# A third PSUM bank for attention scores, and one fewer for transposes, in a two-layer decoder kernel

## The chip, the cores and the metric

The kernel runs on one core of a Trainium2 chip. The time is that of the whole launch on the device, in microseconds (us), the median of the runs shown. The core's engines run side by side, each through its own list of instructions in order, and wait for each other by semaphores: TensorE (PE, matmuls and transposes, writing into PSUM), VectorE (DVE), ScalarE (ACT), GpSimd (POOL) and SyncE (SP, which starts transfers here). PSUM has eight banks of 128 x 512 float32 values; a tile that takes a matmul's result takes one bank.

## The reference

Two layers over 512 tokens of width 1024. Each has one input projection, three token mixers whose results are merged by gates, an output projection and a SwiGLU block. Cut to what is computed:

```python
h = rms_norm(x, mix_norm_g[l])
aq, akc, avc, aks, avs, akw, avw, ag, bcq, bckv, bkpe, cg, cx, ma, mb, mc = split(h @ w_in[l])
# A: 8 heads of 64 in 2 groups; compressed blocks (31), selected blocks, window; merged by gates
o_c = softmax(mask_c(q @ k_c.T)) @ v_c       # k_c, v_c: a small MLP over blocks of 32 tokens
o_s = softmax(mask(q_r @ k_s.T)) @ v_s       # q_r, k_s, k_w carry a rotary embedding
o_w = softmax(mask(q_r @ k_w.T)) @ v_w
ya = g0 * o_c + g1 * o_s + g2 * o_w
# B: latent attention: 8 heads of 96, causal, q and k/v from low-rank bcq and bckv
yb = softmax(mask(q_b @ k_b.T)) @ v_b
# C: causal convolution of cx, gated linear recurrence, times gelu(cg)
merged = sigmoid(ma) * (ya @ w_pa[l]) + sigmoid(mb) * (yb @ w_pb[l]) + sigmoid(mc) * (yc @ w_pc[l])
x = x + merged @ w_o[l]
h = rms_norm(x, ffn_norm_g[l])
x = x + (silu(h @ ffn_w1[l]) * (h @ ffn_w3[l])) @ ffn_w2[l]
```

At 512 tokens there are eight blocks to select from and all are taken, so o_s and o_w are both causal attention over all keys.

## The kernel before

Every large product is float32 made of three passes (`mm3`, lines 111 to 115): both operands are split into a high and a low part, and high x high, high x low and low x high are summed in one PSUM bank. `weights` (103 to 109) loads 128 x 512 values of a matrix into `wr` and splits them: ScalarE writes the high part `wh` (L100), VectorE or, through the attention, GpSimd the low part `wl` (L101).

A layer runs through these stages. First, three **blocks** of projections (`block_tm`): each has four tiles, one per 128 tokens, in banks of the tags t, t, s, s, and sums eight chunks k into all four at once. Between the first block and the next, called block 3 here, `b_in` makes its first product in a "t" tile; four products of its second stand ahead of block 3 and the rest behind it. Block 3's four tiles are read by ScalarE (L422, L413, L414) and VectorE (L423). In block 3, `cmp_mlp` has two groups of 16 small products (L461) for the compressed blocks, the first in a "t" tile, the second in an "mm" tile. The rope tables (first layer only) are made on VectorE (L211 to L229) and end in two sines on ScalarE (L231, L232). The third block, block 1 here, follows.

Then the **attention** (`attn`): 16 jobs of A (a head and a branch each) and 8 of B. Each job has three steps of scores into an "s" tile (`st_s`, L748/L749 for A, L113 to L115 for B), which VectorE masks and reduces (L633) and ScalarE exponentiates (L636); VectorE scales the result (L645); three steps of transposes into a "t" tile (`st_t`, L660), which ScalarE (L100) and VectorE (L101) split into two tiles; and the products with the values into the one "o" bank (`st_v`). The transposes of q and k (`tr4`, L544) and the compressed branch use "t" tiles too. Between the steps, `fill` puts other products in small portions (`b_in`, the gates of A, `b_kv`, `b_halfq`, `merge_a`) into "mm" tiles.

After it (`self.wide = True`) come plain products alone: merge B, the recurrence C, merge C, the output projection and SwiGLU. There `ps()` gives each new "mm" tile the next tag of `WIDE`, so that seven banks are used in turn.

The tags and their banks stand in `pbufs` (line 76): two "mm", two "s", three "t", one "o". A tile waits until a bank of its tag is free, that is until all readers of the tile that had it are done. The order of the instructions on each engine isn't that of the code: a scheduler places them by priority, mostly that of the code, among those that it takes to be ready, so that a change of banks moves instructions.

Of the kernel before, what the change touches and what calls it, by code (L numbers as in the profile page):

```python
# [29 lines left out]
TLAG, VLAG = 6, 2  # L30
EB = 79
F0, F1 = 11.5, 2.5
WIDE = ("s", "t", "mm", "t", "s", "mm", "t")
YK, YQ = 1.3, 1.5
KB = 2
NLAG = 4, 4
# [27 lines left out]
class Builder:  # L64
    def __init__(self, ctx, tc, io, layers=L, dbg=None):
        self.tc, self.nc, self.io, self.layers = tc, tc.nc, io, layers
        self.dbg = dbg or {}
        nc = self.nc
        self.V, self.A, self.T = nc.vector, nc.scalar, nc.tensor
        pool = lambda n, b=1, **k: ctx.enter_context(tc.tile_pool(name=n, bufs=b, **k))  # L70
        self.cst, self.sb, self.sm = pool("cst"), pool("sb"), pool("sm", 2)
        self.psum = pool("psum", 1, space=PSUM)
        self.n = 0
        self.bufs = dict(wr=3, wh=4, wl=4, h=16, mg=8, oT=8, cq=10, qk=8, v=8, big=6, pt=5, P0=2, P1=2, P2=2, P3=3, e=3)
        self.pending = False
        self.pbufs = dict(mm=2, s=2, t=3, o=1)
        self.wide, self.turn = False, 0
        self.weng, self.debt, self.mid = None, 0.0, False

# [7 lines left out]
    def ps(self, tag="mm"):  # L87
        if tag == "mm" and self.wide:
            self.turn += 1
            tag = WIDE[self.turn % 7]  # L90
        return self.psum.tile([128, 512], F32, tag=tag, name=self.nm("ps" + tag), bufs=self.pbufs[tag])
# [1233 lines left out]
```

## Time and profile before

| | us |
|---|---|
| median of 3 runs | 1983.79 (1982.91 to 1984.43) |
| the profiled execution | 1982.81 |
| its span in the trace | 1981.0 |
| TensorE busy | 1935.6 |
| VectorE busy | 1319.7 |
| ScalarE busy | 996.6 |
| GpSimd busy | 252.0 |

The profile is of one execution. The span is the time from the first to the last instruction. Times within the trace count from the span's start. A wait is put down to the instruction that came last among those waited for; idle time of an engine that doesn't set the time costs nothing. The first layer's projections take about 0 to 110 us and its attention goes to about 345; the second layer starts shortly before 1000.

### The profile page before, as it was taken

The page shows a single profiled execution, that of the slowest core. Times are in us where ns is not written, and L with a number is a line of the kernel's source. Part 1 is how long each engine was busy: PE and PEld are TensorE (multiplying, and loading weights), DVE is VectorE, ACT ScalarE, POOL GpSimd, SP SyncE. Part 2 cuts the span into 40 slices and gives each one's busy share as a digit, 9 for nine tenths or more (in the row PEclk, how much of TensorE's full clock was granted, in tenths as well). Part 3 has the DMA queues.
Part 4 walks back from the last instruction along what each step waited for, and adds up shares of the span by engine and source line. Part 5 has one row for each costly group of instructions (what it writes and reads, how often), then busy time and mean ns, then how long its engine had stood idle before and what let it go on. Part 6 is the DMA issues. An engine that isn't in the chain of part 4 may idle for free.

```text
span 1981.0 us, 26967 instructions
## 1 busy us (share of the span) xinstructions
PE 1935.6 (98%) x9472; PEld 1627.8 (82%) x9472; DVE 1319.7 (67%) x2783; ACT 996.6 (50%) x1937; POOL 252.0 (13%) x232
## 2 busy tenths in 40 slices
PE   9898999999999999999999899999999999999999
PEld 8777878888888888888888688888888888888887
DVE  8689998788545554455556999878874465534542
ACT  5466776687334332233344577857773343323331
POOL 0453442000000000000004536310000000000000
PEclk9999999999999999999999999999999999999999
DMA  5211101223333223323432111113233322333333
GB/s 159 86 56 34 41 31 43 87 94 104 109 125 101 96 96 93 99 98 96 131 112 93 43 41 44 38 46 100 95 102 119 121 91 100 96 94 99 97 102 100
DMA packets 100519, 173.94 MB, mean 88 GB/s; under 512 B 11936, under 2 KB 26144, under 8 KB 100384
## 3 DMA queue, kind: packets, MB, share of 16 engines
q1 hardware_dynamic: 100384, 172.22, 27.3%
q8 instruction: 74, 1.21, 0.2%
q14 instruction: 61, 0.50, 0.1%
HBM read 167.98 MB, written 4.19 MB: 87 GB/s over the span
## 4 chain that ended last, share of the span: by engine, by line
PE 78%; DVE 8%; ACT 2%; issue 1%; POOL 0%; ACTq 0%; DVEq 0%; POOLq 0%
PE pst L114 9%; PE pst L113 9%; PE pst L115 9%; PE psmm L113 8%; PE psmm L114 8%; PE psmm L115 8%; PE pss L114 7%; PE pss L113 7%; PE pss L115 7%; PE pst L660 1%; DVE P L645 1%; DVE pss L633 1%; PE pso L673 1%; PE pso L674 1%; ACT P L636 1%
## 5 line engine op out<-in xcount | busy, mean ns | idle before, releaser
L100 ACT ACTIVATE wh<-wr 128x512 fp32r<-128x512 f32 (+3 forms) x640 | 387.5, 608 | 698.4 <-PE pst L114 261.0
L101 DVE TENSOR_TENSOR wl<-wr,wh 128x512 fp32r<-128x512 f32 (+2 forms) x526 | 355.1, 676 | 247.5 <-ACT wh L100 242.4
L101 POOL TENSOR_TENSOR wl<-wr,wh 128x512 fp32r<-128x512 f32 (+2 forms) x114 | 138.8, 1224 | 951.8 <-ACT wh L100 935.8
L113 PE MATMUL psmm<-h,wh 128*128 128x512 f32 x600 | 237.2, 395 | 3.7 <-ACT wh L100 2.8
L115 PE MATMUL psmm<-h,wl 128*128 128x512 f32 x600 | 235.2, 392 | 0.6 <-POOL wl L101 0.6
L114 PE MATMUL psmm<-h,wh 128*128 128x512 f32 x600 | 235.0, 392 | 0.0
L113 PE MATMUL pst<-h,wh 128*128 128x512 f32 x512 | 199.8, 390 | 0.0
L114 PE MATMUL pst<-h,wh 128*128 128x512 f32 x512 | 199.3, 389 | 0.0
L115 PE MATMUL pst<-h,wl 128*128 128x512 f32 x512 | 199.3, 389 | 0.0
L113 PEld LDWEIGHTS psmm<-h,wh 128*128 128x128 f32 x600 | 112.9, 188 | 26.4 <-ACT wh L100 3.2
L113 PE MATMUL pss<-h,wh 128*128 128x512 f32 x344 | 134.2, 390 | 0.0
L115 PE MATMUL pss<-h,wl 128*128 128x512 f32 x344 | 133.9, 389 | 0.0
L114 PE MATMUL pss<-h,wh 128*128 128x512 f32 x344 | 133.9, 389 | 0.0
L115 PEld LDWEIGHTS psmm<-h,wl 128*128 128x128 f32 x600 | 112.9, 188 | 24.6 <-POOL wl L101 1.1
L114 PEld LDWEIGHTS psmm<-h,wh 128*128 128x128 f32 x600 | 112.9, 188 | 20.8
L636 ACT ACTIVATE P<-pss,nm 128x512 f32<-128x512 f32 x192 | 100.1, 525 | 55.4 <-DVE nm L633 32.3
L113 PEld LDWEIGHTS pst<-h,wh 128*128 128x128 f32 x512 | 96.1, 188 | 20.2 <-ACT e L984 0.4
L115 PEld LDWEIGHTS pst<-h,wl 128*128 128x128 f32 x512 | 96.1, 188 | 20.1
L114 PEld LDWEIGHTS pst<-h,wh 128*128 128x128 f32 x512 | 96.1, 188 | 19.8
L633 DVE CUSTOM_DVE_ANT_0 pss<-pss,mask 128x512 f32<-128x512 f32 x192 | 93.7, 489 | 7.2 <-PE pss L115 5.8
L660 PE MATMUL pst<-ident,P 128*128 128x128 f32 x480 | 76.6, 274 | 11.5 <-DVE P L645 5.3
L660 PEld LDWEIGHTS pst<-ident,P 128*128 128x128 f32 x480 | 58.2, 141 | 28.1 <-issue 17.8
(423 smaller groups left out, 4303.4 us busy)
## 6 DMA issues: line engine op xcount, KB each, us to landing
wr<-w SPq DMA_DIRECT2D x240, 256.0 KB, 2.6
wr<-wfm SPq DMA_DIRECT2D x188, 256.0 KB, 2.6
wr<-wpc SPq DMA_DIRECT2D x32, 256.0 KB, 2.6
wr<-wo SPq DMA_DIRECT2D x32, 256.0 KB, 2.6
wr<-wb SPq DMA_DIRECT2D x32, 192.0 KB, 2.4
wr<-w SPq DMA_DIRECT2D x32, 192.0 KB, 2.3
mg<-xT SPq DMA_DIRECT2D x16, 256.0 KB, 2.7
wr<-wpa SPq DMA_DIRECT2D x16, 256.0 KB, 2.6
```

Source lines behind the costliest of these rows:

```text
L100: self.A.activation(hi, src, AF.Copy)
L101: (eng or self.V).tensor_tensor(lo, src, hi.bitcast(F32), OP.subtract)
L113: mm(ps, a[0], b[0], start=first, stop=False)
L114: mm(ps, a[0], b[1], start=False, stop=False)
L115: mm(ps, a[1], b[0], start=False, stop=last)
L633: self.V.tensor_tensor_reduce(p[:, :W], p[:, :W], self.mask[:, 512 - W:], 1.0, 3e38, OP.add, OP.min, j.nm[:, i:i + 1])
L636: self.A.activation(j.Pi[i], p[:, :128 * (i + 1)], AF.Exp, bias=j.nm[:, i:i + 1], scale=-1.0, accum_out=j.l[:, i:i + 1])
L645: V.tensor_scalar(j.Pi[i], j.Pi[i], j.gate[:, i:i + 1], j.l[:, i:i + 1], op0=OP.mult, op1=OP.mult)
L660: self.T.transpose(ps[:, c:c + 128], j.Pi[i][:, kt * 128:kt * 128 + 128], self.ident)
L673: T.matmul(o[:, 512 - n:], j.V[kt], h[:, m0:m0 + n], start=j.first and kt == 0, stop=False)
L674: T.matmul(o[:, 512 - n:], j.V[kt], l_[:, m0:m0 + n], start=False, stop=j.last and kt == NT - 1)
```

## The change

One "t" bank becomes an "s" bank, and the walk over the banks for plain products is written for the new numbers (three s, two t, two mm in seven).

```diff
-WIDE = ("s", "t", "mm", "t", "s", "mm", "t")
+WIDE = ("s", "t", "mm", "s", "t", "mm", "s")
...
-        self.pbufs = dict(mm=2, s=2, t=3, o=1)
+        self.pbufs = dict(mm=2, s=3, t=2, o=1)
```

The number of matmuls, evictions and loads stays the same. What moves is their order. On TensorE at the start of block 3 in the first layer (582 to 585 are its tiles, wh_587/wl_588 the weights of its chunk 0, wh_608/wl_609 those of chunk 1; a line with - is the order before, with + the order after):

```order
 L114 MATMUL pst_582<-wl_609,h_121 128x312
 L115 MATMUL pst_582<-wh_608,h_122 128x312
+L113 MATMUL pss_584<-wh_608,h_121 128x312
+L113 MATMUL pst_583<-wh_587,h_79 128x312
+L114 MATMUL pst_583<-wl_588,h_79 128x312
+L115 MATMUL pst_583<-wh_587,h_80 128x312
 L113 MATMUL pst_583<-wh_608,h_121 128x312
 L114 MATMUL pst_583<-wl_609,h_121 128x312
 L115 MATMUL pst_583<-wh_608,h_122 128x312
-L113 MATMUL pss_584<-wh_608,h_121 128x312
 L114 MATMUL pss_584<-wl_609,h_121 128x312
```

The three products of pst_583 with chunk 0 stood right behind those of pst_582 with chunk 0; now they stand behind chunk 1's products of pst_582 and one of pss_584, with 13 matmuls of block 3 ahead of them. The second layer has the same move.

On TensorE behind block 3, among the products of b_in's second tile (psmm_550), the group of the compression product (two rows of eight matmuls, L461):

```order
 L115 MATMUL psmm_550<-h_129,wl_553 128x512
 L113 MATMUL psmm_550<-h_137,wh_552 128x512
+L461 MATMUL pst_686<-pt_475,qk_682 64x62 x8
+L461 MATMUL pst_686<-pt_476,qk_683 64x62 x8
 L114 MATMUL psmm_550<-h_138,wh_552 128x512
 L115 MATMUL psmm_550<-h_137,wl_553 128x512
```

Before, it stood in the middle of block 3, behind chunk 3; now it is behind the whole block and four further products. The second layer has this move too.

On ScalarE around the evictions of block 3, first layer (v, gth and kpe are what ScalarE reads out of the tiles 582 to 585; big_382 and big_384 are the sines of the rope tables; wh_926 and wh_942 are splits of weights for TensorE's next products):

```order
 L465 ACTIVATE cth_787<-psmm_770 64x62
-L231 ACT_TABLE_LOAD
-L231 ACTIVATE big_382<-big_380 128x192
 L100 ACTIVATE wh_926<-wr_925 128x512
-L232 ACTIVATE big_384<-big_380 128x192
-L100 ACTIVATE wh_942<-wr_941 128x384
 L422 ACTIVATE v_832<-pst_582,ny_360 128x4x64
 L422 ACTIVATE v_837<-pst_583,ny_360 128x4x64
-L100 ACTIVATE wh_961<-wr_960 128x384
 L422 ACTIVATE v_842<-pss_584,ny_360 128x4x64
 L413 ACTIVATE gth_830<-pst_582,ny_360 128x24
+L100 ACTIVATE wh_942<-wr_941 128x384
```

The sines stood ahead of the weight splits and evictions; now they stand behind all of them (and so does wh_961). On VectorE, the evictions of block 3 (L423) stood behind L229, the last step of the rope tables' angle; now the first of them stands six steps (L226) ahead of it.

## Rows read from the trace of the kernel before

**Rows 1.** The page's first part: busy us (share of the span) x instructions

```profile
PE 1935.6 (98%) x9472; PEld 1627.8 (82%) x9472; DVE 1319.7 (67%) x2783; ACT 996.6 (50%) x1937; POOL 252.0 (13%) x232
```

**Rows 2.** Busy time by stretch: stretch and us; PE, PEld, DVE, ACT, POOL; clock; DMA

```profile
200.00:250.00 50.00, 47.44 (x289) 42.60 (x287) 49.39 (x158) 37.01 (x98) 25.06 (x27) 1.00 0.13 40
...
400.00:450.00 50.00, 50.00 (x223) 41.40 (x222) 42.40 (x66) 40.40 (x62) 0.00 (x0) 1.00 0.29 97
```

**Rows 3.** Waits of TensorE: engine, line, waited for; us in total, times, longest

```profile
PE pss L748 <- ACT P L636: 10.6, 13, 1.4
```

**Rows 4.** Busy time by stretch, the two attentions

```profile
110.00:300.00 190.00, 171.93 (x1019) 145.54 (x1017) 184.18 (x550) 132.77 (x352) 82.98 (x77) 0.99 0.12 38
1095.00:1250.00 155.00, 144.06 (x842) 122.62 (x841) 147.05 (x464) 105.98 (x277) 76.92 (x71) 0.99 0.14 44
```

**Rows 5.** Timeline, first layer, block 3: start, us, instruction, count [idle before <-releaser]

```profile
43.25 0.30 PE L113 MATMUL pst<-wh,h 128*128 128x312 f32 x1
...
49.02 0.69 DVE L339 TENSOR_TENSOR e<-pst,rsb 128x512 f32<-128x512 f32 x1
...
55.89 2.08 PE L461 MATMUL psmm<-pt,qk 128*64 128x62 f32 x32
```

**Rows 6.** Timeline, first layer, between block 3 and block 1's end

```profile
66.87 0.35 DVE L226 SCALAR_TENSOR_TENSOR big<-pt,big 128x192 f32<-128x192 f32 x1
67.25 0.26 DVE L229 TENSOR_SCALAR big<-big 128x192 f32<-128x192 f32 x1
...
67.55 0.36 ACT L231 ACTIVATE big<-big 128x192 f32<-128x192 f32 x1 [8.02 <-DVE big L229]
...
68.48 0.50 PE L113 MATMUL psmm<-h,wh 128*128 128x512 f32 x1 [2.81 <-ACT wh L100]
...
70.89 0.34 PE L113 MATMUL pst<-wh,h 128*128 128x384 f32 x1
...
85.20 0.33 PE L113 MATMUL pst<-wh,h 128*128 128x384 f32 x1
...
93.52 0.39 PE L113 MATMUL psmm<-h,wh 128*128 128x512 f32 x1
```

**Rows 7.** Busy time by stretch, first layer, block 1

```profile
70.00:75.00 5.00, 3.04 (x12) 2.17 (x13) 4.93 (x12) 2.85 (x12) 2.10 (x3) 0.94 0.41 120
75.00:80.00 5.00, 5.00 (x22) 4.85 (x22) 4.35 (x9) 3.71 (x8) 1.65 (x2) 0.72 0.13 39
```

**Rows 8.** Timeline, second layer, block 3 to block 1

```profile
1035.97 0.30 PE L113 MATMUL pst<-wh,h 128*128 128x312 f32 x1
...
1041.66 0.69 DVE L339 TENSOR_TENSOR e<-pst,rsb 128x512 f32<-128x512 f32 x1
...
1042.69 0.31 PE L115 MATMUL pss<-wh,h 128*128 128x312 f32 x1
...
1054.09 0.39 PE L113 MATMUL psmm<-h,wh 128*128 128x512 f32 x1
...
1057.94 0.39 PE L115 MATMUL psmm<-h,wl 128*128 128x512 f32 x1
...
1058.82 0.86 DVE L423 SCALAR_TENSOR_TENSOR v<-pst,ny,v 128x256 fp32r<-128x256 f32 x2
...
1059.92 0.28 ACT L414 ACTIVATE kpe<-pst,ny 128x32 f32<-128x32 f32 x1
...
1060.28 0.34 PE L113 MATMUL pst<-wh,h 128*128 128x384 f32 x1
...
1061.16 0.44 PE L114 MATMUL pst<-wl,h 128*128 128x384 f32 x1 [0.54 <-POOL wl L101]
...
1068.37 0.44 PE L114 MATMUL pst<-wl,h 128*128 128x384 f32 x1 [0.50 <-POOL wl L101]
```

**Rows 9.** Timeline, first layer, one transpose group and VectorE's end of its eviction

```profile
137.28 0.60 PE L660 MATMUL pst<-ident,P 128*128 128x128 f32 x4
...
142.13 0.63 DVE L101 TENSOR_TENSOR pt<-pst,pt 128x512 fp32r<-128x512 f32 x1
```

## The prediction

> **What bounds the kernel now.** I read the profile from the whole to the place. The page's busy line puts TensorE at 98% of the span [rows 1], so over the whole kernel little but TensorE's own work sets the time. The stages differ, though. In 50 us stretches TensorE is full in the plain products (400 to 450) and not in the attention (200 to 250), where VectorE is busy for 49.39 of 50 us [rows 2]. The attention runs from about 110 to 300 in the first layer and 1095 to 1250 in the second. Over these stretches VectorE is busy for 184.18 of 190 and 147.05 of 155 us, TensorE for 171.93 and 144.06 [rows 4]. So **VectorE carries the attention**: 5.8 and 8.0 us are all that it leaves idle there, while TensorE has 18.1 and 10.9 us to spare. What the change aims at is a line in the list of TensorE's waits: score matmuls (L748) that wait for the exponential (L636) to leave a score bank, 13 times, 10.6 us in all [rows 3].
>
> Ahead of the attention stand three blocks of projections per layer, each in two "t" and two "s" banks. There the order of work shows what the missing third "t" bank does, so the sum is made there.
>
> **The change, part by part.** *Nothing is added or taken away in work*: the same matmuls, evictions and loads run in the same number. The walk over seven banks for plain products meets each bank every seventh tile before and after, and TensorE's order in those stages differs in bank names alone. I cost that part at nothing. Its cover is that each eviction there has six other tiles' time; a walk out of step with its pools would be seen as waits in the stretch that is now 50.00 of 50 us busy [rows 2].
>
> *First wait, block 3.* The tile of b_in's first product (pst_506) and block 3's first two (pst_582, pst_583) had a "t" bank each. With two banks pst_583 must take the one that pst_506 leaves, so its first products now stand behind 13 others. In the first layer block 3 starts at 43.25; a 312-column matmul goes out every 0.143 us (48 from 1035.97 to 1042.69 with the last) [rows 5, 8], so TensorE is there at 43.25 + 13 x 0.143 = 45.1. VectorE reads pst_506 (L339) only at 49.02 and ends at 49.71 [rows 5], as it does its earlier work first in both orders. TensorE waits 4.6 us. In the second layer: there at 1037.8, free at 1041.66 + 0.69 = 1042.35 [rows 8], 4.5 us.
>
> *Second wait, the compression product.* Its group (L461, 2.08 us [rows 5]) had the third bank in the middle of block 3. It now stands behind block 3 and four products of b_in, and needs a bank that block 3 leaves, which is when ScalarE has read the tile for the last time (L414). TensorE gets there, first layer: 49.7 + 83 x 0.143 + one other L461 group of 2.1 + 4 x 0.227 = 64.6; the 0.227 us is from 17 matmuls between 1054.09 and 1057.94 [rows 8]. VectorE's own eviction (L423) comes before ScalarE's last read and has its place six steps of the rope tables (0.36 us each) ahead of L229, which ran at 67.25 [rows 6]: at 65.1 if nothing else moves, at about 68 if the ten small steps now put ahead no longer run between the others. I take 67, nearer to the upper end since those steps depend on each other, plus 1.3 for the eviction, the two reads and a weight split between them on ScalarE. So the group starts at 68.3, after 3.7 us, and the next block (block 1) at 68.3 + 2.1 + 20 x 0.227 = 74.9, where it started at 70.89 [rows 6]: 4.0 later.
>
> *What the first layer gets back.* ScalarE waited 8.02 us for VectorE's angle (L231) with weight splits and evictions queued behind it, and TensorE waited 2.81 us for one of these [rows 6]. In the new order L231 stands behind the evictions. Block 1 took 93.52 - 70.89 = 22.6 us, and at the pace of its undisturbed second half (48 matmuls from 85.20 to 93.52 [rows 6], 0.173 each) 96 take 16.6: 6.0 us of waits and low clock, which the later start gives its weights time to avoid. Of these, 1.7 us are clock: 0.94 and 0.72 of full over two stretches of 5 us, the lower of the two levels for part of them, right after TensorE's waits [rows 7]. A new wait of 3.7 us may bring that again. First layer: 4.0 - 6.0 = -2.0 without, -0.3 with it. I take 0, since that nothing else waits in block 1 is the best case.
>
> *The second layer gets nothing back*, as no rope tables are made there. VectorE's evictions start at 1058.82, ScalarE's last read of the tile ends at 1059.92 + 0.28 [rows 8]; both orders have the same work ahead of them. TensorE is there at 1042.35 + 83 x 0.143 + 2.2 + 0.9 = 1057.3, waits to 1060.2, and starts block 1 at 1060.2 + 2.1 + 4.5 = 1066.8 instead of 1060.28. Waits of 0.54 and 0.50 us in block 1 fall away [rows 8]: **+5.5 us**, or +7.2 with a stretch of low clock. VectorE has nothing to do while block 1 runs, so the whole attention moves by that much.
>
> *The third score bank.* Its bounds are far apart. All 10.6 us of [rows 3] at best; nothing if VectorE is the limit, since a score that is ready sooner is read no sooner; and a loss if two banks hold the transposes back. The nearest row is VectorE's idle time, 5.8 and 8.0 us [rows 4], most of it many short handovers that a bank doesn't shorten. I take -2 for both layers, bounds -10.6 and +8 (the rivals).
> The Trainium skill, page "Perfetto Trace Analysis", section "Identifying Performance Opportunities", speaks against the change: work on the engine that is most contended within the regime, which here is VectorE by [rows 4]. By that rule alone the score bank brings 0 and the sum would be 1989.
>
> **The sum.** 0 + 5.5 - 2 = +3.5 us on the profiled execution of 1982.81 (span 1981.0), 1986.3. The median of the runs, 1983.79, is 1.0 above it, so I forecast **1987** us.
>
> **Rivals.** (a) *The score bank is what TensorE lacks.* All 10.6 us go and the blocks still lose 5.5: 1983.8 - 5.1 = 1978.7. For it: 13 waits on just that bank. Against it: VectorE's 97 and 95%. It decides when VectorE's busy share in the attention rises above these.
> The same page and section of the Trainium skill has the rule for this: gaps that repeat on the engine that should be saturated can mean too little PSUM for the next tile. The trace has the gaps, but on an engine that is not the saturated one there.
>
> (b) *Two banks are too few for the transposes: slower.* Place: the attention of both layers. A transpose group holds its bank from its start on TensorE to the end of VectorE's subtraction (L101), 137.28 to 142.76 in one case, 5.5 us [rows 9]. Three groups per job and about one further "t" tile share two banks, and 16 jobs fill the 190 us, 11.9 each. Up to 2 x 11.9 / 4 = 6.0 us of mean hold cost nothing; above it each 0.1 us lengthens a job by 0.2. At 6.3 that is 0.6 a job, and for about half of 32 jobs 9 us: 1987 + 9 = 1996. For it: 5.5 is close to 6.0. Against it: in the order the transposes move by few places, and holds among the later heads, where VectorE has room, must be shorter.
>
> (c) *The blocks don't lose.* If the evictions of pst_506 and pst_582 come earlier than I place them, the two waits are hidden: 1983.8 - 2 = 1982.
>
> **How the numbers follow.** Chances: forecast 0.50 (its own range 1983 to 1991), (a) 0.18, (b) 0.20, (c) 0.12. A measurement tells 0.2% from no change, 4 us: faster ends at 1979.8, slower begins at 1987.8. Slower: (b) and 0.21 of the forecast, 0.41. Faster: most of (a), 0.16. Same: 0.43. Range: from just under (a) to (b), 1978 to 1996, which leaves about 2 in 10 out.
>
> **What would show it.** Right: TensorE waits of some 4.5 us for L339 in block 3 of both layers; a wait of 2 to 4 us ahead of an L461 group behind block 3; block 1 of the first layer in under 20 us; block 1 of the second layer starting some 6 us later within its layer; the score waits shorter than 10.6 us with VectorE's busy time in the attention and the attention's length nearly as before. Wrong: an attention shorter by more than 5 us in a layer (a), new TensorE waits of transposes (L660, L544) for L101 (b), or no wait in block 3 (c).

## The result, and the profile after

The changed kernel takes **1997.12 us** (median of 4 runs, 1992.99 to 1999.29), the kernel before 1983.94 on the same chip: a ratio of 1.0061 [1.0049, 1.0073], 12 us slower. The forecast was 1987 with a range up to 1996; the time lies 1.1 us above the range. "No change" had a chance of 0.43 and "slower" 0.41; it was slower.

The profiled execution took 1999.29 us, the longest of the four, with a span of 1997.5 us. The busy line of its page, against [rows 1]:

```profile
PE 1948.9 (98%) x9472; PEld 1640.9 (82%) x9472; DVE 1314.7 (66%) x2783; ACT 998.7 (50%) x1937; POOL 253.6 (13%) x232
```

The number of TensorE's instructions is the same and its busy time is 13.3 us longer: products ran for longer. With that goes TensorE's mean granted clock, which fell from 0.997 to 0.989. Its waits (engine, line, waited for; us in total, times, longest), of which [rows 3] showed one line:

```profile
PE pst L660 <- DVE pt L101: 12.6, 8, 3.7
PE pst L113 <- DVE e L339: 8.4, 2, 4.5
PE pst L461 <- ACT kpe L414: 3.0, 1, 3.0
```

The score waits (10.6 us) are gone: no wait of L748 for L636 of 0.3 us or more is left in TensorE's list, as the change meant. In their place stand transposes that wait for VectorE's split (L101), the two waits of block 3 for L339 and one of the compression group for L414.

Busy time by stretch (us; PE, PEld, DVE, ACT, POOL; clock; DMA), the two attentions 7 and 13 us later than in [rows 4], and the 5 us around the end of the wait of block 3 (51.03) or behind it (1049.50):

```profile
117.00:307.00 190.00, 175.47 (x1019) 148.71 (x1018) 180.91 (x550) 134.60 (x352) 83.09 (x77) 0.96 0.12 38
1108.00:1263.00 155.00, 143.01 (x824) 122.43 (x823) 142.60 (x452) 103.77 (x269) 76.76 (x71) 0.97 0.14 44
50.00:55.00 5.00, 3.96 (x15) 3.97 (x16) 4.97 (x23) 2.17 (x4) 0.96 (x2) 0.50 0.07 14
1050.00:1055.00 5.00, 5.00 (x21) 5.00 (x20) 4.58 (x15) 1.65 (x4) 1.70 (x2) 0.50 0.11 32
```

In the first stretch VectorE runs the same 550 instructions and is busy for 3.3 us less; in the second it gets through 452 instead of 464. It is idle for more of the time than before, not less. Where block 3 goes on after its wait the granted clock is 0.50, the lower of the two levels.

The timeline of TensorE and ScalarE shows the path from block 3 to block 1 (start, us, instruction, count, idle before and its releaser), first layer and then second. These are single rows that answer to [rows 5, 6, 8]; others lie between them:

```profile
44.48 0.30 PE L113 MATMUL pst<-wh,h 128*128 128x312 f32 x1
51.03 0.63 PE L113 MATMUL pst<-wh,h 128*128 128x312 f32 x1 [4.53 <-DVE e L339]
70.86 0.28 ACT L414 ACTIVATE kpe<-pst,ny 128x32 f32<-128x32 f32 x1
71.19 2.74 PE L461 MATMUL pst<-pt,qk 128*64 128x62 f32 x32 [3.02 <-ACT kpe L414]
79.42 0.33 PE L113 MATMUL pst<-wh,h 128*128 128x384 f32 x1
88.15 0.44 PE L114 MATMUL pst<-wl,h 128*128 128x384 f32 x1 [2.12 <-POOL wl L101]
100.08 0.39 PE L113 MATMUL psmm<-h,wh 128*128 128x512 f32 x1
...
1043.62 0.30 PE L113 MATMUL pst<-wh,h 128*128 128x312 f32 x1
1049.50 0.63 PE L113 MATMUL pst<-wh,h 128*128 128x312 f32 x1 [3.85 <-DVE e L339]
1067.03 0.30 ACT L414 ACTIVATE kpe<-pst,ny 128x32 f32<-128x32 f32 x1
1067.38 2.08 PE L461 MATMUL pst<-pt,qk 128*64 128x62 f32 x32
1074.07 0.33 PE L113 MATMUL pst<-wh,h 128*128 128x384 f32 x1
```

Cutting the trace at the first product of block 3, the first of block 1 and the first score job (L748) gives the stages. The first table line is worked out from 43.25, 70.89 and 113.11 (first layer) and 1035.97, 1060.28 and 1088.74 (second) in the trace of before; the others in the same way from their own traces. "Attention" runs from the first score job to the last product with the values; the plain products, from there to the next block 3 or to the last product, are 691.3 to 691.8 and 654.6 to 655.6 us long in every kernel. What comes ahead of block 3 differs by up to 1.6 us between executions with the same order on TensorE.

| kernel | ratio to before [interval] | block 3 to block 1, layers 1, 2 | block 3 to first score, 1, 2 | attention, 1, 2 |
|---|---|---|---|---|
| before | 1 | 27.6, 24.3 | 69.9, 52.8 | 231.2, 233.2 |
| changed | 1.0061 [1.0049, 1.0073] | 34.9, 30.5 | 75.6, 56.7 | 231.9, 237.5 |
| e1, no late bank in the blocks | 1.0004 [0.9995, 1.0013] | 29.9, 24.5 | 70.2, 52.4 | 230.4, 237.7 |
| e2, six banks | 1.0051 [1.0039, 1.0064] | 34.5, 30.8 | 75.2, 57.0 | 231.9, 236.0 |
| e3, six banks, blocks as e1 | 1.0015 [1.0006, 1.0024] | 30.0, 24.2 | 70.3, 52.2 | 232.8, 237.6 |
| e4, a pool of five | 1.0007 [0.9998, 1.0015] | 27.7, 24.3 | 69.9, 52.8 | 230.3, 235.4 |
| e5, products in the first wait | 1.0060 [1.0048, 1.0073] | 34.7, 32.3 | 75.4, 58.6 | 231.9, 235.0 |
| e6, first wait undone | 1.0073 [1.0060, 1.0086] | 35.1, 33.5 | 75.8, 59.7 | 230.3, 234.9 |
| e7, second wait undone | 1.0040 [1.0027, 1.0052] | 30.2, 30.2 | 72.1, 56.5 | 231.5, 237.5 |
| e8, before, splits on VectorE | 0.9975 [0.9964, 0.9985] | 28.5, 24.3 | 66.2, 52.7 | 231.0, 233.2 |
| e9, changed, splits on VectorE | 1.0038 [1.0026, 1.0051] | 32.8, 30.2 | 69.4, 56.5 | 231.8, 237.4 |
| e10, as e8 in both layers | 0.9979 [0.9970, 0.9988] | 28.6, 24.4 | 66.3, 52.3 | 232.5, 232.8 |
| e11, e1 and e8 | 0.9990 [0.9982, 0.9999] | 29.1, 24.3 | 68.3, 52.3 | 231.0, 235.0 |
| e12, e4 and e8 | 0.9985 [0.9977, 0.9994] | 28.6, 24.3 | 66.3, 52.7 | 230.6, 236.2 |

From before to the changed kernel the blocks lose 5.7 and 3.9 us, the attention 0.7 and 4.3 us in this one profile, whose execution was the longest of the four.

### The profile page after: what moved, and what is told of

Read it like the earlier page. It is cut to its first block, busy times and chain, and to the rows that moved or that the text cites. A ratio compares the mean times of both kernels' runs of the same rounds, so it can differ in the third digit from the quotient of the medians.

```text
span 1997.5 us, 26963 instructions
## 1 busy us (share of the span) xinstructions
PE 1948.9 (98%) x9472; PEld 1640.9 (82%) x9472; DVE 1314.7 (66%) x2783; ACT 998.7 (50%) x1937; POOL 253.6 (13%) x232
## 4 chain that ended last, share of the span: by engine, by line
PE 83%; DVE 13%; ACT 2%; issue 1%; DMA 1%; POOL 0%; SPq 0%; ACTq 0%; DVEq 0%; POOLq 0%
PE pss L114 10%; PE pss L115 10%; PE pss L113 10%; PE psmm L114 9%; PE psmm L113 9%; PE psmm L115 9%; PE pst L113 7%; PE pst L114 7%; PE pst L115 7%; PE pst L660 2%; DVE P L645 2%; DVE pss L633 1%; PE pso L673 1%; PE pso L674 1%; DVE pt L101 1%
## 5 line engine op out<-in xcount | busy, mean ns | idle before, releaser
L101 DVE TENSOR_TENSOR wl<-wr,wh 128x512 fp32r<-128x512 f32 (+2 forms) x526 | 353.5, 673 | 249.4 <-ACT wh L100 244.5
L101 POOL TENSOR_TENSOR wl<-wr,wh 128x512 fp32r<-128x512 f32 (+2 forms) x114 | 140.5, 1236 | 964.8 <-ACT wh L100 961.6
L115 PE MATMUL psmm<-h,wl 128*128 128x512 f32 x600 | 237.6, 396 | 0.0
L113 PE MATMUL pss<-h,wh 128*128 128x512 f32 x488 | 190.0, 389 | 0.0
L115 PE MATMUL pss<-h,wl 128*128 128x512 f32 x488 | 189.9, 389 | 0.0
L114 PE MATMUL pss<-h,wh 128*128 128x512 f32 x488 | 189.8, 389 | 0.0
L113 PE MATMUL pst<-h,wh 128*128 128x512 f32 x368 | 143.8, 391 | 0.4 <-ACT v L100 0.3
L115 PE MATMUL pst<-h,wl 128*128 128x512 f32 x368 | 143.2, 389 | 0.0
L114 PE MATMUL pst<-h,wh 128*128 128x512 f32 x368 | 143.2, 389 | 0.0
L636 ACT ACTIVATE P<-pss,nm 128x512 f32<-128x512 f32 x192 | 100.1, 526 | 54.6 <-DVE nm L633 19.5
L115 PEld LDWEIGHTS pss<-h,wl 128*128 128x128 f32 x488 | 91.6, 188 | 19.0
L114 PEld LDWEIGHTS pss<-h,wh 128*128 128x128 f32 x488 | 91.6, 188 | 18.9
L113 PEld LDWEIGHTS pss<-h,wh 128*128 128x128 f32 x488 | 91.6, 188 | 19.0
L660 PE MATMUL pst<-ident,P 128*128 128x128 f32 x480 | 79.4, 281 | 20.4 <-DVE pt L101 12.6
L660 PEld LDWEIGHTS pst<-ident,P 128*128 128x128 f32 x480 | 57.4, 143 | 43.2 <-DVE pt L101 16.9
```

The source lines that it names most:

```text
L101: (eng or self.V).tensor_tensor(lo, src, hi.bitcast(F32), OP.subtract)
L113: mm(ps, a[0], b[0], start=first, stop=False)
L114: mm(ps, a[0], b[1], start=False, stop=False)
L115: mm(ps, a[1], b[0], start=False, stop=last)
L636: self.A.activation(j.Pi[i], p[:, :128 * (i + 1)], AF.Exp, bias=j.nm[:, i:i + 1], scale=-1.0, accum_out=j.l[:, i:i + 1])
L660: self.T.transpose(ps[:, c:c + 128], j.Pi[i][:, kt * 128:kt * 128 + 128], self.ident)
```

## The experiments

Theory 1 was that the blocks carry the loss, theory 2 that two transpose banks in the attention do. The first four kernels tell these apart.

**e1: the late tiles get a score bank.**

```diff
-            ps = self.ps("mm" if z else "t")
+            ps = self.ps("mm" if z else "s")
...
-... self.gemm_gen(self.win(l, nme, c), self.h, "t" if t0 else "mm")
+... self.gemm_gen(self.win(l, nme, c), self.h, "s" if t0 else "mm")
```

> The changed kernel, but b_in's first tile and the first compression group take the third score bank instead of a transpose bank, so that TensorE's order around block 3 is again that of the kernel before; the attention keeps three score banks and two for transposes. Theory 1 (the blocks carry the loss): in the profile of the changed kernel the stretch from block 3's start to the first score job is 5.7 us longer in the first layer and 3.9 us in the second; both go, so 1997.1 - 9.6 = 1987.5 us, no wait for L339 in block 3. Theory 2 (two transpose banks in the attention carry it): the waits of L660 for L101 (12.6 us in the changed kernel) stay and the time is 1993 us or more. If the third score bank is worth its 10.6 us beneath the block loss: under 1980 us.

Measured: 1986.9 us, 1.0004 [0.9995, 1.0013]. The time lies at the value of theory 1 (1987.5). Two tags bring back 0.57% or some 11 us of the loss; 0.04% is left. The attention still has three score and two transpose banks, and the waits of its transposes are those of the changed kernel:

```profile
PE pst L660 <- DVE pt L101: 12.5, 8, 3.7
PE psmm L113 <- ACT wh L100: 2.7, 1, 2.7
PE pst L660 <- DVE P L645: 2.5, 1, 2.5
```

So theory 1 holds and theory 2 falls: the 12.5 us of new waits are there without the 12 us of loss. A smaller loss in the attention isn't excluded by this; e3 and e11 bear on it.

**e2: two score and two transpose banks, the eighth idle until the plain products.**

```diff
-WIDE = ("s", "t", "mm", "s", "t", "mm", "s")
+WIDE = ("s", "t", "mm", "x", "s", "t", "mm")
...
-        self.pbufs = dict(mm=2, s=3, t=2, o=1)
+        self.pbufs = dict(mm=2, s=2, t=2, x=1, o=1)
```

> The changed kernel with two score banks and two transpose banks: the eighth bank stands idle until the plain products behind the attention, which still walk over seven. It differs from the changed kernel only in the third score bank. If that bank is worth nothing (VectorE carries the attention): 1995 to 1999 us, as the changed kernel, and the waits of L748 for L636 come back. If it is worth what those waits sum to before: about 1997.1 + 10.6 = 2007.7 us. If it does harm by letting scores run ahead of transposes: under 1993 us.

Measured: 1995.62 us, 1.0051 [1.0039, 1.0064], against 1.0061 with the third score bank: no difference that can be told, so the first case holds for the time. Its other half doesn't: the score waits did not come back to 10.6 us; 2.6 us of L748 for L636 remain, while transposes wait for L101 for 10.9 us.

**e3: six banks, and the late tiles in the idle eighth.** The edit is that of e2 with "x" for the two tags of e1.

> As the one with six banks, but b_in's first tile and the first compression group take the idle eighth bank, so the order around block 3 is that of the kernel before, and the attention has two score banks and two for transposes. Against the kernel before it shows what the third transpose bank is worth in the attention alone; against the first experiment, what the third score bank is worth there. Theory 1: within 3 us of the first experiment, 1985 to 1990 us. Theory 2: 1993 us or more, and waits of L660 for L101 above 10 us. If the third score bank makes up for a lost transpose bank: 5 us or more above the first experiment.

Measured: 1988.69 us, 1.0015 [1.0006, 1.0024]. Against the kernel before, the attention has lost a transpose bank and got nothing for it: 3.0 us. Against e1 it has a score bank less: 0.11%, 2.2 us, but the intervals overlap, and e2 against the changed kernel gave 0.10% the other way. What a third score bank is worth next to two transpose banks is some 2 us either way by these two, not told from nothing.

**e4: one pool of five banks for scores, transposes and blocks** (every "t" becomes "s", `s=5`).

> Scores, transposes and the block tiles draw on one pool of five banks instead of three and two (or two and three). If it is the fixed split of the banks that costs the time, neither wait remains: no wait for L339 in block 3, under 3 us of L748 for L636, under 3 us of L660 for L101, and 1978 to 1984 us. If the scores, being first in the code, run ahead and hold banks that transposes need: waits of L660 for a score's exponential (L636) above 10 us, and 1992 us or more. If VectorE alone sets the attention: 1983 to 1987 us whatever the waits.

Measured: 1987.1 us, 1.0007 [0.9998, 1.0015]. The waits for banks shrink to 3.4 us (L748 for L636) and 2.7 us (L660 for L101), near what the first case expected of them, but the time isn't the first case's 1978 to 1984 us. It is that of the third, 1983 to 1987, to 0.1 us. Other waits take the place of those for banks. TensorE's largest waits now, against [rows 3]:

```profile
PE pss L660 <- DVE P L645: 7.6, 2, 3.9
PE pss L748 <- ACT P L636: 3.4, 6, 1.0
```

These are waits for VectorE's results, not for a bank. No split of the five banks that was tried makes the attention shorter by an amount that can be measured.

The next three take the blocks' loss apart.

**e5: TensorE works through the first wait.** In block 3's first chunk the tile that waits comes last, and 32 unread products stand ahead of it.

```diff
-            for i in range(NT):
+            late = k == 0 and N == N3
+            for i in (0, 2, 3, 1) if late else range(NT):
...
+                if late and i == 1:
+                    po = self.ps("o")
+                    for _ in range(32):
+                        self.T.matmul(po[:, :N], hh[:, ts], w[0], start=True, stop=True)
```

> The changed kernel with 32 unread 128x312 products (into the free 'o' bank, about 32 x 0.143 = 4.6 us) put into TensorE's order just ahead of pst_583's first product in block 3 of both layers; nine products of the block stand ahead of them (13 in the changed kernel). The wait for VectorE's L339 is as long as before, but TensorE works through it, so that only what follows the wait can change. In the changed kernel the 5 us behind that wait have a granted clock of 0.50 and 0.50, and the products go out every 0.26 instead of 0.143 us until about 4.5 us later: 2.2 us lost per layer. Theory A (the low clock behind a wait is a cost of its own): granted clock 1.00 there, block 3 about 2.2 - 0.6 = 1.6 us shorter in each layer, 1997.1 - 3.2 = 1993.9 us or, if the next wait also keeps its clock, down to 1992. Theory B (the lost clock is hidden by what VectorE and ScalarE do next): 1996 to 1999 us.

Measured: 1998.32 us, 1.0060 [1.0048, 1.0073]: theory B. The clock did what theory A said of it. Busy time by stretch in this kernel, the same 5 us as above and the 5 us behind the next wait:

```profile
50.00:55.00 5.00, 5.00 (x37) 5.00 (x36) 5.00 (x28) 2.14 (x5) 2.01 (x3) 1.00 0.15 37
70.00:75.00 5.00, 5.00 (x36) 4.61 (x36) 2.81 (x10) 2.40 (x10) 0.81 (x2) 0.50 0.14 41
```

In the first stretch the clock is 1.00 instead of 0.50, and 37 products go out in 5 us instead of 15 (the changed kernel waited for the first of these 5 us). Behind the next wait the clock is at 0.50. Block 1 starts 34.7 and 32.3 us after block 3, no sooner than in the changed kernel (34.9, 30.5). The second layer, which had no wait at the compression group, now has one of 2.52 us. What TensorE won in block 3 it gave back waiting for the same read of ScalarE. The run doesn't take the low clock away, it moves it from the first wait to the second.

**e6: only b_in's first tile gets a score bank** (the second half of e1's edit).

> The changed kernel, but b_in's first tile takes a score bank; the compression group keeps its transpose bank and stays late. The wait for L339 in block 3 and its low clock go. Theory: in the first layer the second wait takes nearly all of it, since block 3's readers on VectorE run at the same time whenever TensorE is done, so TensorE waits there 3.0 + 4.5 = 7.5 us and block 1 starts at most 2 us sooner than in the changed kernel; in the second layer block 3 is 4.5 us shorter and the wait for L414 returns with 2.9 us, 1.6 sooner. Time 1997.1 - 1.6 - (0 to 2) = 1993.5 to 1995.5 us. Rival (the two waits add up, each with its own cost): first layer 4.5 + 2.2 us, second 4.5 us sooner, 1986 to 1988 us.

Measured: 2000.29 us, 1.0073 [1.0060, 1.0086]. My expectation (1993.5 to 1995.5) was too low and the rival's far too low: without its first wait the kernel is, if anything, slower. Timeline of the second layer, ScalarE's read and TensorE's compression group:

```profile
1066.11 0.28 ACT L414 ACTIVATE kpe<-pst,ny 128x32 f32<-128x32 f32 x1
...
1066.43 3.67 PE L461 MATMUL pst<-pt,qk 128*64 128x62 f32 x32 [3.49 <-ACT kpe L414]
```

Block 3 starts at 1042.10 here, so the read comes 24.0 us behind it; in the changed kernel it came 1067.03 - 1043.62 = 23.4 us behind, and before 1059.92 - 1035.97 = 23.95 [rows 8]. So this read comes at nearly the same time in all three, whether block 3's products end 18 us (before), 20 (e6) or 23 us (changed) behind its first; it is VectorE's and ScalarE's earlier work that sets it. TensorE gets there sooner, waits 3.49 us, and the low clock behind this wait falls on the group, which takes 3.67 instead of 2.08 us, and on the products behind it, all of them ahead of block 1.

**e7: only the first compression group gets a score bank** (the first half of e1's edit).

> The changed kernel, but the first compression group takes a score bank and stands early in block 3 again; b_in's first tile keeps its transpose bank, so block 3 still waits for L339. Theory: in the first layer block 3 is still 4.5 us late but the wait for L414 and its low clock go (3.0 + 1.7 us), so block 1 starts as in the first experiment or up to 1 us later; in the second layer, where that wait was nearly nil in the changed kernel, nothing is won. Time 1997.1 - 5 = 1992 us (1990.5 to 1993.5). Rival (the two waits are one loss, the second only the echo of the first): no change, 1996 to 1998 us.

Measured: 1993.81 us, 1.0040 [1.0027, 1.0052], 0.3 us above the expected 1990.5 to 1993.5, and by layers as expected: in the first layer block 1 starts 30.2 us behind block 3, as in e1 (29.9), although block 3 still waits for L339; in the second layer nothing is won (30.2 against 30.5). So in the first layer the group's place is what delays block 1, and the first wait costs next to nothing beside VectorE's chain. In the second layer either alone is enough to delay it, by 5.9 us here and by 9.2 in e6: with the first wait, block 3 itself takes 24.6 us between its first and last products instead of 18.0; with the second, the group is late.

The last five go after the step that the prediction took as given back. (GpSimd makes the low parts of the weights from block 3 on, not only through the attention: `self.weng` is set ahead of block 3.)

**e8: the kernel before, with block 1's low parts in the first layer on VectorE.**

```diff
+        self.weng = None if l == 0 else nc.gpsimd
         for k in self.steps(self.block_tm(io["wb12"][l, 1], N12)):
             self.step()
...
+        self.weng = nc.gpsimd
         raw1 = self.a_raw(self.ret)
```

(The expectations of e8, e9, e11 and e12 count block 1 to its last chunk, half a microsecond shorter than the 22.6 us of the prediction; the texts here count as the prediction did, to the first product behind it.)

> The kernel before (three transpose banks, two score banks), with the low parts of block 1's eight weight chunks in the first layer made on VectorE instead of GpSimd. In the kernel before TensorE waits 1.60 us for GpSimd's part there, block 1 takes 22.1 us in the first layer and 17.9 in the second, and VectorE is busy for 0.28 of 5 us from 82 to 87. The prediction took block 1's 6.0 us of waits as what a later start can give back; the changed kernel gave back 2.0. If GpSimd's part is what keeps block 1 long: 16.6 to 18.5 us for block 1 and 1980 to 1982 us. If VectorE's own earlier work delays the low parts instead: TensorE waits for VectorE's L101 in their place and the time is 1984 us or more.

Measured: 1980.85 us, **0.9975 [0.9964, 0.9985]**, as expected if GpSimd's part keeps block 1 long, and faster than both kernels of the change. Block 1 takes 18.1 us (71.67 to 89.80) instead of 22.6.

**e9: the changed kernel with the same edit.**

> The changed kernel with the low parts of block 1's weights in the first layer made on VectorE instead of GpSimd. In the changed kernel block 1 of the first layer starts 7.3 us late against block 3's start and gives back 2.0 us (20.1 us instead of 22.1), with a wait of 2.12 us for GpSimd's part and a stretch of low clock behind it left in it. If GpSimd's part is why the start's delay was not given back: block 1 takes 16.6 to 17.6 us and the time is 1997.1 - 3 = 1994 us (1993 to 1995). If the later start has already taken what can be had: 1996 us or more.

Measured: 1992.85 us, 1.0038 [1.0026, 1.0051], 0.23% or some 4.5 us under the changed kernel. Block 1 takes 16.66 us, which is the undisturbed 16.6 of the prediction. By the table the first score comes 6.2 us sooner behind block 3 than in the changed kernel; 4.0 of these are block 1, and 2.2 come ahead of it, where the compression group waits 2.63 us and then takes 2.08 us instead of 2.74. The edit thus moved more than block 1. TensorE's timeline, block 1's first product and the first one behind it:

```profile
77.34 0.33 PE L113 MATMUL pst<-wh,h 128*128 128x384 f32 x1
...
94.00 0.39 PE L113 MATMUL psmm<-h,wh 128*128 128x512 f32 x1
```

Busy time by stretch, the 15 us inside it: TensorE without a gap and at full clock.

```profile
78.00:93.00 15.00, 15.00 (x89) 15.00 (x88) 9.80 (x23) 4.78 (x9) 1.45 (x2) 1.00 0.30 93
```

Against e8 the exchange of banks still costs 0.63%, about what it costs with these splits on GpSimd (0.61%). So GpSimd's part is why block 1 gave little back, but not why the exchange costs time.

**e10: as e8, in both layers** (`self.weng = None` without the condition).

> The kernel before with the low parts of block 1's weights on VectorE in both layers. In the second layer of the kernel before TensorE waits twice for GpSimd's part there, 0.54 and 0.50 us, and VectorE is idle from 1067.5 to 1082. If those waits are the price: 1 us less than with VectorE in the first layer alone (0.9975 of the kernel before), a ratio of 0.997. If VectorE's eviction and rotation steps come first there and hold the low parts back: 0.9975 to 0.999.

Measured: 1980.22 us, 0.9979 [0.9970, 0.9988]: not told from e8, in the range of the second case and not the 0.997 of the first. From block 3 to the first score the second layer is 0.4 us shorter in the table, less than the 1 us expected.

**e11: e1 and e8 together.**

> Three score banks and two transpose banks, b_in's first tile and the compression group in a score bank (the first experiment), with the low parts of block 1's weights of the first layer on VectorE. The first experiment stood at 1.0004 of the kernel before, and block 1 took 19.8 us there. If the two edits add: block 1 takes 16.6 to 17.6 us, 2 to 3 us less, a ratio of 0.9985. If the third score bank is worth more once block 1 is short: under 0.9975.

Measured: 1983.66 us, 0.9990 [0.9982, 0.9999]. The time is near the 0.9985 of edits that add, but block 1 takes 19.2 us, or 18.7 as the expectation counts, and not 16.6 to 17.6. Against e8, which differs in the banks alone, three score banks and two transpose banks are 0.15% or 3 us slower, with intervals that just overlap; the first layer's blocks are 2.1 us longer and the second's attention 1.8 us.

**e12: e4 and e8 together.**

> One pool of five banks for scores, transposes and blocks, with the low parts of block 1's weights of the first layer on VectorE. The pool alone stood at 1.0007 of the kernel before with block 1 at 22.1 us there. If the edits add: block 1 at 17.6 us, 4.5 us less, 0.998. If the pool wins with the VectorE splits over three and two fixed banks: under 0.9965.

Measured: 1982.96 us, 0.9985 [0.9977, 0.9994], where "the edits add" put 0.998; block 1 takes 18.1 us, 4.5 less than in e4, as put. This pool doesn't beat the fixed banks.

## Why the prediction was wrong, point by point

**What bounds the kernel** held as far as these runs show. The plain products' length did not move, so the walk costs nothing, and the score waits went without a gain.

**The first wait, block 3.** Forecast 4.6 and 4.5 us; measured 4.53 and 3.85 us, for L339 as named. The sum rightly did not count these waits by themselves but the start of block 1; e5 and e6 show that this was needed, since neither filling nor removing the wait starts block 1 sooner while the group is late.

**The second wait and the late group.** This is the cause, and its working had the right chain: VectorE's chain, ScalarE's last read, then the group and 20 products, which before lay ahead of that read and now lie behind it, on the path to block 1. Second layer: forecast 30.8 us from block 3 to block 1 (1066.8 - 1035.97), measured 30.45. The forecast wait of 2.9 us ahead of the group isn't there, though: the low clock in block 3, which the sum left out, brought TensorE to the group some 2.4 us later than forecast, just as the read ended. As the read set the start, that cost nothing, and with full clock there the wait is back (2.52 us in e5). First layer: forecast 74.9 - 43.25 = 31.65, measured 34.94, so 3.3 too little. Of these, 1.66 are the group's start (26.7 us behind block 3, forecast 25.05; the term was "I take 67" plus 1.3), 0.66 the group itself (2.74 for 2.08) and 1.0 the 20 products (73.93 to 79.42, 5.5 for 4.5). The last two are the low clock behind the wait, by this stretch:

```profile
73.90:75.90 2.00, 2.00 (x6) 1.61 (x6) 0.48 (x3) 1.41 (x3) 0.61 (x1) 0.53 0.03 8
```

The sum took every product at full clock, and counted a low one only as a possible loss inside block 1. The late start of the group is VectorE's: its first eviction of block 3 (L423) runs at 69.76, 25.28 us behind block 3's start, where the 67 put 23.75 and its upper end 24.75. Two small steps ahead of it stand out, each beside a split on GpSimd:

```profile
62.43 1.27 POOL L101 TENSOR_TENSOR wl<-wr,wh 128x512 fp32r<-128x512 f32 x1 [0.69 <-ACT wh L100]
62.54 1.19 DVE L287 TENSOR_SCALAR pp<-pp 128x8 f32<-128x8 f32 x1
66.35 1.34 POOL L101 TENSOR_TENSOR wl<-wr,wh 128x512 fp32r<-128x512 f32 x1 [2.65 <-ACT wh L100]
66.45 1.28 DVE L467 TENSOR_SCALAR chid<-chid 64x62 f32<-64x62 f32 x1
```

The same steps take 0.17 and 0.18 us elsewhere, so 2.1 us went there. Before, GpSimd was idle from 58.5 to 68.5, behind ScalarE's wait for L229; in the changed order these splits run beside VectorE's chain. No run moves them off GpSimd, so their share isn't tested.

**What the first layer gets back** is a step that failed in its mechanism. The prediction let block 1 fall from 22.6 to 16.6 us, or to 18.3 with 1.7 us of low clock; it took 100.08 - 79.42 = 20.7 us, 2.0 less than before. Of the 6.0 us before, the larger waits inside block 1 were one for ScalarE's last read of block 3 and one for GpSimd's low part:

```profile
73.24 0.45 PE L113 MATMUL pst<-wh,h 128*128 128x384 f32 x1 [1.66 <-ACT kpe L414]
...
83.18 0.44 PE L114 MATMUL pst<-wl,h 128*128 128x384 f32 x1 [1.60 <-POOL wl L101]
```

The first went, with the low clock behind it, as forecast. The second grew to 2.12 us, and now it has low clock behind it. The 5 us behind it, before and then changed:

```profile
83.20:88.20 5.00, 5.00 (x29) 5.00 (x30) 0.00 (x0) 1.05 (x2) 2.96 (x4) 1.00 0.49 131
88.20:93.20 5.00, 5.00 (x20) 5.00 (x21) 0.00 (x0) 0.52 (x1) 2.84 (x3) 0.66 0.46 131
```

GpSimd's rows in the changed kernel show why, one split of 384 columns in block 1 and a later one:

```profile
82.59 5.51 POOL L101 TENSOR_TENSOR wl<-wr,wh 128x384 fp32r<-128x384 f32 x1 [2.88 <-ACT wh L100]
91.71 1.01 POOL L101 TENSOR_TENSOR wl<-wr,wh 128x384 fp32r<-128x384 f32 x1 [1.68 <-ACT wh L100]
```

Beside the slow one, VectorE was busy for 4.65 of 5 us; beside the other for none, by the busy time of these stretches:

```profile
82.60:87.60 5.00, 3.43 (x20) 3.11 (x18) 4.65 (x10) 1.05 (x2) 5.00 (x1) 1.00 0.00 0
91.70:92.70 1.00, 1.00 (x4) 1.00 (x4) 0.00 (x0) 0.00 (x0) 0.99 (x1) 0.50 0.48 174
```

The kernel before has the same at this place. Its long split on GpSimd and VectorE's last step (L796), then that step in the changed kernel:

```profile
79.82 3.31 POOL L101 TENSOR_TENSOR wl<-wr,wh 128x384 fp32r<-128x384 f32 x1 [3.35 <-ACT wh L100]
82.00 0.28 DVE L796 TENSOR_TENSOR qc<-cosb,gB 128x128 f32<-128x128 f32 x1
...
86.97 0.28 DVE L796 TENSOR_TENSOR qc<-cosb,gB 128x128 f32<-128x128 f32 x1
```

The split ends 0.85 us behind VectorE's last step in both. The prediction named ScalarE's queue as what held block 1, and lumped GpSimd's wait with what a later start avoids. A later start doesn't avoid it, as VectorE's steps move too: L796 ends 39.0 us behind block 3's start before and 42.8 behind it in the changed kernel. e9 shows that the 6.0 us were really there: with these splits off GpSimd block 1 took 16.66 us. The Trainium skill, page "Perfetto Trace Analysis", section "Optimizing Scalar/DVE Operations", says that GpSimd and VectorE share a read port of SBUF, so that moving work between the two might not help. The row agrees with the sharing; what followed here is that the work was better off on VectorE alone.

In the first layer the blocks thus lost 5.7 us where 0 stood: 3.3 are the start of block 1 beyond the forecast, and 2.4 are what was not given back of the 4.0 that the 0 counted on.

**The second layer** was forecast at +5.5 and lost 3.9 us: block 1 starts 6.1 us later (6.5 forecast) and gives back 2.2 us on the way to the first score (1.04 forecast).

**The third score bank** was set at -2 us. e1 puts the whole exchange in the attention, a score bank for a transpose bank, at +0.8 us (-1.0 to +2.6), e11 against e8 at +3.0. The score bank's own share is some 2 us either way, not told from nothing. What the sum left out is the lost transpose bank, 3.0 us by e3 (1.2 to 4.8); the prediction had it only as rival (b), at nothing or 9 us. The wait that (b) named is there; its largest, in the second layer's attention of the changed kernel:

```profile
1138.89 1.11 PE L660 MATMUL pst<-ident,P 128*128 128x128 f32 x4 [3.71 <-DVE pt L101]
```

With two fixed transpose banks the second layer's attention is 1.7 to 4.5 us longer than before in every profile; in the two others with three, e8 and e10, it is within 0.4 us. The first layer's moves by 1.6 us at most, both ways.

**The rivals.** (a) fell: 10.6 us of score waits went and nothing was gained. (b) gave nearly the right time, 1996, by luck and for the wrong reason: e1 keeps its waits and loses next to nothing. (c) fell: the blocks lost.

**The sum.** Forecast 0 + 5.5 - 2 = +3.5. The blocks measure 5.7 + 3.9 = 9.6 us in the profile and 11 us in the runs (the changed kernel against e1), the attention about +1 to +3: 12 us in all. Against the sum, the first layer's blocks were 5.7 us too low, the second's 1.6 too high, and the bank's term 3 to 5 too low. The range was too narrow at its upper end because it let the first layer's blocks cost no more than nothing. They had no bound above that, though two of their terms, the 67 and the 6.0, were best cases or choices.

## What to carry to other kernels

A bank taken from a pool is paid for by every tile that used it, not only in the stage that the change looks at: here the attention hardly noticed, and two tiles of the projections cost the 11 us. When a wait moves work, ask on which side of the next fixed event (here ScalarE's read of block 3, set by VectorE) the work ends up; work that slipped behind it here cost nearly its full length (6.1 of 6.6 us in the second layer), and a wait that ended before it cost nothing (e7, first layer). A gain that is "given back" needs the same proof as a gain: find out what holds the stage now, and move that (here one engine for eight splits, 0.25%).

## What the runs showed of the hardware

A GpSimd subtraction of 128 x 384 values that takes 1.01 us took 5.51 us while VectorE worked beside it with hardly a gap: VectorE's last instruction there ends at 87.25, GpSimd's at 88.10, 0.85 us later. So it looks as if nearly all of the work was done after VectorE had fallen idle. The same holds in all nine kernels that leave these splits on GpSimd (before, changed, e1 to e7): the long one takes 3.3 or 5.5 us, and ends 0.84 to 0.86 us behind VectorE's last instruction. It goes the other way too: VectorE's small L287 and L467 took 1.19 and 1.28 us beside a GpSimd split instead of 0.17 and 0.18, and ended 0.03 and 0.04 us behind it (63.73 against 63.70, 67.73 against 67.69).

The clock's fall behind a wait cost time in these runs only where TensorE's next products were on the path: in block 3 it took products from 0.143 to 0.26 us each and e5, which avoided it there, was no faster; ahead of block 1 in e6 it made the compression group 1.6 us longer. Not every such wait brought it: in e9 the group took its 2.08 us behind a wait of 2.63. The changed kernel has more such stretches in its attention than the kernel before, and so does e1 (mean clock 0.993 against 0.997), which is no slower.
